# GLA diagonal as a product of q and k summed by matmuls with ones, output projection side by side, FFN groups of 16

## The chip, the cores and the metric

One core of a Trainium2 chip. The metric is the time of one execution on the device, in microseconds (us). TensorE (PE) does matmuls, VectorE (DVE) and ScalarE (ACT) element work, GpSimd (POOL) a few fills and a DMA queue, SyncE (SP) the main DMA queue.

## The reference

One layer of a hybrid decoder on x of 512 tokens and width 2048, in float32:

```python
h = rmsnorm(x); parts = split(h @ w_in)      # three head groups read the same h
mix = concat(gmlp(..), diff_attention(..), gla(..))   # 512 + 768 + 768
x = x + mix @ w_out
gate, up = split(rmsnorm(x) @ w_ffn_in)      # hidden width 5632
x = x + (silu(gate) * up) @ w_ffn_out
y = rmsnorm(x)

def gla(q, k, v, ...):                       # 4 heads, dk = 96, dv = 192, chunks of 64
    g = log_sigmoid(gate_code @ gate_w2 + gate_b) / 16
    b = cumsum(g)                            # inside a chunk
    A[i, j] = sum_d q[i, d] * k[j, d] * exp(b[i, d] - b[j, d])   # j <= i
    S = diag(exp(b_last)) @ S + (k * exp(b_last - b)).T @ v
    o = (q * exp(b)) @ S_before + A @ v
```

On the diagonal, i = j, the exponential is 1, and A[i, i] is the plain sum of q[i, d] * k[i, d] over d.

## The kernel before

Activations lie transposed, features on partitions and the 512 tokens along the row. Each float32 factor of a large product is split into a high part rounded to the fp32r format (a cast on ACT) and a low rest (a subtraction on DVE). `mm3` then makes three fp32r matmuls of each step: hi with hi, hi with lo, lo with hi.

The stages follow each other on PE. First comes the input projection (`wsr`, `wsg`, `wsd`, `b` and others are its PSUM tiles), between whose matmuls the mixers are woven in: each GLA head (`gla(h)`) and each attention head is a generator, and `pe.tick()` runs the next piece of one when the PE time estimated since its last `yield` is over. PE takes its instructions in the order in which this program writes them while `pe.held` is set. A piece's operations on ACT and DVE are written at the same point, and those queues are in order too.

In `gla(h)`, `z` is the gate's product on PE. ACT makes `ab` from it in three steps (Abs, Exp, Ln), DVE forms `pre` from `ab` and clears `suf`. After `yield 4.0` come the four matmuls of `A{h}d`, 128x128 each, of k against q: only their diagonals are used, picked into `at` by a predicated copy. Then `factors` doubles a step size from 1 to 256; its first exp is `c` from `pre`, its product with q or k is on DVE, and its sums go into `suf` and `pre`. q and k themselves are the tiles `gqk`.

The output projection (`wo_half`) runs over two halves of T (th), 16 blocks n of 128 outputs, and two halves of the 16 blocks k of `mix`; its weights are split into `wh_o` and `wl_o`, its operands are `mxs`, the split `mix`. `wo_out` adds x and keeps the sum. The loads of x for it go over SP's queue. The first LEAD = 4 blocks n have their first weight half done ahead.

The first FFN product uses a scheme with 7 products in place of 8 (`sx`, `bx`, `bz` and the like are PSUM tiles of it and of the next). The second runs over 44 hidden blocks in five parts: `rest` over 3, `second` over a group of 14, `rest` over 3, `second` over another 14, and `last` over 10. `second` makes, for each of 8 pairs q of output blocks, 7 products, each a sum over 7 pairs of hidden blocks at 3 matmuls of 256 columns. `last` takes its blocks plainly, for 10 output blocks n at 512 columns and for the last 6 in two halves of 256. `load_ops(g)` loads and splits the operands of a group, which were stored in DRAM by the first product.

Of the kernel before, what the change touches and what calls it, by code (L numbers as in the profile page):

```python
# [16 lines left out]
P = 128  # L17
# [7 lines left out]
GP = 7  # L25
R0 = (0, 1, 2)
S0 = 3
R1 = (31, 32, 33)
S1 = 17
R2 = tuple(range(34, 44))  # L30
KORDER = [*R0, *range(S0, S0 + 14, 2), *range(S0 + 1, S0 + 14, 2), *R1, *range(S1, S1 + 14, 2),
          *range(S1 + 1, S1 + 14, 2), *R2]
# [13 lines left out]

def group_of(j):
    return 0 if S0 <= j < S0 + 14 else 1 if S1 <= j < S1 + 14 else None
# [40 lines left out]
def trunk_kernel(  # L89
# [86 lines left out]
    def square_x(k):  # L176
        xt = mix[:, k]
        if k == 0:
            act.activation(sqa, xt, AF.Square)
        else:  # L180
            sq = t2(f"sq{k}")
            act.activation(sq, xt, AF.Square)
            dve.tensor_add(sqa, sqa, sq)

    def xstat(src, width, blocks, evac, name, first=False):
        for b, (c0, cw) in enumerate(blocks):
# [4 lines left out]
            for kn in steps:  # L191
# [22 lines left out]
                if first and k0 in (8, 16):  # L214
                    for k in range(k0 - 8, k0):
                        square_x(k)
# [72 lines left out]
    for h in (1, 2, 4, 8, 16, 32, 64):  # L289
# [9 lines left out]
        masks[h] = m  # L299
    one1 = mp.tile([P, 1], F32, name="one1")  # L300
# [66 lines left out]
    def gla(h, q, k):  # L367
# [12 lines left out]
        dve.memset(suf, 0.0)  # L380
        yield 4.0
# [5 lines left out]
        qh, kh = q[:DK], k[:DK]  # L387
        pa = ps(f"A{h}d")
        for i in range(4):
            sl = slice(i * P, i * P + P)  # L390
            sx = slice((i ^ 2) * P, (i ^ 2) * P + P)
            pe.matmul(pa[:, sl], lhsT=kh[:, sl], rhs=qh[:, sx], start=True, stop=True)
# [275 lines left out]
    mxs = operand("mxs")  # L668

    def split_mix(ks):  # L670
        for k in ks:
            hi, lo = (mxs[w][SLOT[k] // 8][:, SLOT[k] % 8] for w in range(2))
            act.copy(hi, mix[:, k])
            dve.tensor_sub(lo, mix[:, k], hi.bitcast(F32))

    wob, wqs = {}, []

    def wo_half(n, th, hf):
        hs = HALF[th]
        if hf == 0:  # L680
            wob[n] = big.tile([P, T], F32, tag="b", name=f"wo{n}_{th}")[:, :TH]
        wh, wl = split_w(wout[n, hf].rearrange("p k c -> p (k c)"), 1024, f"o{n}_{th}{hf}",
                         None if hf == 0 or pe.held else wqs[0].tile([P, 1024], F32, tag="raw", bufs=3, name=f"w2o{n}_{th}"))
        for kk in range(8):
# [4 lines left out]
            mm3(wob[n], wh[:, c], wl[:, c], mxs[0][k // 8][:, k % 8, hs], mxs[1][k // 8][:, k % 8, hs],  # L689
                i == 0, i == KT - 1)  # L690
# [15 lines left out]
    wqs.append(wq)  # L706
# [35 lines left out]
    def rms2(th):  # L742
# [7 lines left out]
             9: lambda: op_pair(2, b21)}  # L750
    def wo_out(n, th):
        hs = HALF[th]
        xr = wq.tile([P, 4, TH], F32, tag="s", bufs=2, name=f"xr{n}_{th}")
        nc.sync.dma_start(xr[:, 0], xT[:, n, hs])
        xn = xr[:, 0]
        dve.tensor_add(xn, wob[n], xn)
# [8 lines left out]
    for th in range(2):  # L765
        for n in range(0 if th else LEAD, KT):
            if th == 0 and n == LEAD:
                for m in range(LEAD):
                    wo_half(m, 0, 1)
                    wo_out(m, 0)  # L770
            if th == 1 and n in early:
                early[n]()
            for hf in range(2):
                wo_half(n, th, hf)
            wo_out(n, th)
# [75 lines left out]
    class Unit(Products):  # L851
        def __init__(self, j):
# [8 lines left out]
            pr, pos = (j + 1) // 2, (j + 1) % 2  # L861
# [50 lines left out]
        def p4(self):  # L912
# [9 lines left out]
            elif (self.j + 1) % 2:  # L922
# [50 lines left out]
    def load_rest(js):  # L973
        for i, j in enumerate(js):
            st = stage()
            pool.dma_start(st, actd[j])
            if len(js) == 3:
                hi, lo = ([fops[PORDER[2 * i + w]][:, 7, h] for h in range(2)] for w in range(2))
            else:
                hi, lo = (fops[PORDER[e // 8]][:, e % 8] for e in (2 * i, 2 * i + 1))  # L980
                act.copy(hi, st)
                dve.tensor_sub(lo, st, hi.bitcast(F32))
                acts[j] = (hi, lo)
                continue
            for h in range(2):
                act.copy(hi[h], st[:, h])
                dve.tensor_sub(lo[h], st[:, h], hi[h].bitcast(F32))
# [240 lines left out]
```

## Time and profile before

| | |
|---|---|
| three runs | 2123.96, 2125.35, 2126.82 us; median 2125.35 |
| profiled execution | 2125.52 us, span 2123.5 us, mean granted clock 0.997 |
| busy share of the span | PE 99%, DVE 75%, ACT 50%, POOL 5% |

The span is the stretch from the first to the last recorded work; the execution's own time has some 2 us more around it. Busy PE counts matmuls alone; their weight loads are shown apart (PEld) and run beside them. The granted clock is a share of TensorE's full speed.

### The profile page before, as it was taken

To read this page: it belongs to the slowest core of one execution; us is meant where nothing else is said; L and a number is where in the kernel's file an instruction comes from. 1 tells how busy PE (TensorE), PEld (TensorE's weight loads), DVE (VectorE), ACT (ScalarE), POOL (GpSimd) and SP (SyncE) were. 2 spreads that over 40 slices of the span, in tenths; PEclk is the share of its full clock that TensorE was granted. 3 is DMA by queue.
4 is the path that set the end of the run, shared out by engine and by line. 5 is a ranking of instruction groups with operands and counts; after the bars stand their busy time and mean duration, and the time that the engine had idled before them with its cause. 6 is when DMAs were issued, how large, how long until landed. Compare 5 with 4: busy or idle time off the path is not lost.

```text
span 2123.5 us, 33149 instructions
## 1 busy us (share of the span) xinstructions
PE 2104.5 (99%) x13210; PEld 1911.7 (90%) x13210; DVE 1584.0 (75%) x2181; ACT 1059.7 (50%) x1505; POOL 100.8 (5%) x186
## 2 busy tenths in 40 slices
PE   9999999999999999999999999999999999999997
PEld 8988899888899999888888888888888999999987
DVE  6444655566565779988988888888888788888646
ACT  6334455566655555445445544444546533433444
POOL 3000000000000000000000000000001100100000
PEclk9999999999999999999999999999999999999999
DMA  6332223222277765344444334334335644633436
GB/s 211 85 108 80 73 74 92 70 75 74 80 231 231 228 196 160 124 136 135 148 134 143 125 120 145 126 122 134 115 110 169 201 137 143 202 105 105 116 99 191
DMA packets 94683, 284.33 MB, mean 134 GB/s; under 512 B 11089, under 2 KB 29697, under 8 KB 94529
## 3 DMA queue, kind: packets, MB, share of 16 engines
q1 hardware_dynamic: 81728, 236.88, 36.0%
q0 software_dynamic: 11584, 44.57, 6.2%
q8 instruction: 104, 1.70, 0.3%
q10 hardware_dynamic: 1216, 0.76, 0.1%
q14 instruction: 51, 0.41, 0.1%
HBM read 256.74 MB, written 25.43 MB: 133 GB/s over the span
## 4 chain that ended last, share of the span: by engine, by line
PE 95%; DVE 2%; issue 1%; ACT 1%; DMA 1%; DVEq 0%; POOL 0%; POOLq 0%; ACTq 0%
PE bx L67 21%; PE bz L67 11%; PE wo L67 8%; PE sx L67 8%; PE wsd L67 6%; PE by L67 5%; PE wsg L67 4%; PE sz L67 4%; PE fb_None L67 3%; PE b L67 3%; PE c L67 3%; PE rb L67 2%; PE a L67 2%; PE wsr L67 2%; PE fb L67 2%; PE sy L67 2%
## 5 line engine op out<-in xcount | busy, mean ns | idle before, releaser
L67 PE MATMUL bx<-op,fh 128*128 128x512 f32 x1344 | 478.0, 395 | 0.0
L67 PE MATMUL bx<-op,fl 128*128 128x256 f32 x1344 | 379.3, 282 | 0.4 <-DVE fl L805 0.4
L67 PEld LDWEIGHTS bx<-op,fh 128*128 128x128 f32 x1344 | 252.4, 188 | 58.8
L804 ACT CAST fh<-s 128x1024 fp32r<-128x1024 f32 x168 | 177.0, 1053 | 197.6 <-PE by L67 63.8
L67 PEld LDWEIGHTS bx<-op,fl 128*128 128x128 f32 x1344 | 253.1, 188 | 0.8 <-DVE fl L805 0.8
L67 PE MATMUL bz<-op,fh 128*128 128x512 f32 x672 | 240.5, 396 | 0.0
L805 DVE TENSOR_TENSOR fl<-s,fh 128x1024 fp32r<-128x1024 f32 x168 | 204.5, 1218 | 47.9 <-ACT fh L804 47.9
L804 ACT CAST fh<-f 128x1024 fp32r<-128x1024 f32 x126 | 132.5, 1052 | 170.0 <-PE bx L67 85.9
L67 PE MATMUL bz<-op,fl 128*128 128x256 f32 x672 | 189.5, 282 | 0.2 <-DVE fl L805 0.2
L67 PE MATMUL wo<-mxs,wh_o 128*128 128x256 f32 x1024 | 184.1, 283 | 0.0
L805 DVE TENSOR_TENSOR fl<-f,fh 128x1024 fp32r<-128x1024 f32 x126 | 153.7, 1220 | 16.7 <-ACT fh L804 16.7
L67 PE MATMUL sx<-fop,wh_s 128*128 128x256 f32 x896 | 162.0, 282 | 0.0
L67 PEld LDWEIGHTS wo<-mxs,wh_o 128*128 128x128 f32 x1024 | 158.5, 190 | 0.1
L67 PEld LDWEIGHTS bz<-op,fh 128*128 128x128 f32 x672 | 126.2, 188 | 30.5
L67 PE MATMUL wo<-mxs,wl_o 128*128 128x256 f32 x512 | 144.9, 283 | 2.0 <-DVE wl_o L152 2.0
L67 PEld LDWEIGHTS sx<-fop,wh_s 128*128 128x128 f32 x896 | 137.9, 189 | 0.2 <-issue 0.2
L67 PEld LDWEIGHTS bz<-op,fl 128*128 128x128 f32 x672 | 126.7, 188 | 0.5 <-DVE fl L805 0.5
L67 PE MATMUL sx<-fop,wl_s 128*128 128x256 f32 x448 | 126.1, 281 | 0.0
L67 PE MATMUL wsd<-xs,wh_d 128*128 128x512 f32 x384 | 122.9, 401 | 0.0
L67 PE MATMUL by<-op,fh 128*128 128x512 f32 x336 | 119.9, 397 | 0.0
L67 PEld LDWEIGHTS wo<-mxs,wl_o 128*128 128x128 f32 x512 | 97.2, 190 | 2.2 <-DVE wl_o L152 2.2
L67 PE MATMUL by<-op,fl 128*128 128x256 f32 x336 | 94.2, 280 | 0.0
(406 smaller groups left out, 4769.5 us busy)
## 6 DMA issues: line engine op xcount, KB each, us to landing
f<-wf SPq DMA_DIRECT2D x168, 512.0 KB, 3.9
w_o<-wout SPq DMA_DIRECT2D x32, 512.0 KB, 4.2
w2o<-wout SPq DMA_DIRECT2D x32, 512.0 KB, 3.9
sraw<-wf SPq DMA_DIRECT2D x32, 448.0 KB, 3.9
sw<-wf SPq DMA_DIRECT2D x32, 448.0 KB, 4.2
opd<-tmp POOLq DMA_DIRECT2D x14, 896.0 KB, 4.1
w_d<-wst SPq DMA_DIRECT2D x24, 512.0 KB, 3.5
w_g<-wst SPq DMA_DIRECT2D x16, 512.0 KB, 3.5
```

What stands on the lines that cost most here:

```text
L67: self.note(self.tc.nc.tensor.matmul(out, lhsT=lhsT, rhs=rhs, **k), out, rhs)
L804: act.copy(wh, a)
L805: dve.tensor_sub(wl, a, wh.bitcast(F32))
```

## The change

There are three parts and some small ones. In each GLA head the diagonal becomes an elementwise product: DVE multiplies k and q into `ab`, ACT casts that to `qkh`, DVE subtracts to get the rest `qkl`, and two fp32r matmuls of 512 columns with a matrix of ones (`onesr`) sum each over the 96 partitions. In the output projection hi and lo of an operand lie beside each other, so that one matmul of 512 columns does hi with hi and hi with lo in two halves of a PSUM tile, and one of 256 does lo with hi; `wo_out` adds both halves. Its loads of x go to POOL's queue, one turn ahead. In the second FFN product the groups have 16 blocks instead of 14, and `last` 6 instead of 10; operands and weights lie in other buffers for it. The squares of x at the start are made in smaller portions and kept in program order.

```diff
-GP = 7
+GP = 8
 R0 = (0, 1, 2)
 S0 = 3
-R1 = (31, 32, 33)
-S1 = 17
-R2 = tuple(range(34, 44))
-KORDER = [*R0, *range(S0, S0 + 14, 2), *range(S0 + 1, S0 + 14, 2), *R1, *range(S1, S1 + 14, 2),
-          *range(S1 + 1, S1 + 14, 2), *R2]
+R1 = (19, 20, 21)
+S1 = 22
+R2 = tuple(range(38, 44))
+KORDER = [*R0, *range(S0, S0 + 16, 2), *range(S0 + 1, S0 + 16, 2), *R1, *range(S1, S1 + 16, 2),
+          *range(S1 + 1, S1 + 16, 2), *R2]
...
+SQUARES = {4: (0, 3), 6: (3, 6), 8: (6, 8), 10: (8, 10), 12: (10, 12), 14: (12, 14), 16: (14, 16)}
...
-                if first and k0 in (8, 16):
-                    for k in range(k0 - 8, k0):
-                        square_x(k)
+                for k in range(*SQUARES.get(k0, (0, 0)) if first else (0,)):
+                    square_x(k)
...
+    onesr = mp.tile([P, P], F32R, name="onesr")
+    act.activation(onesr, ident, AF.Copy, scale=0.0, bias=1.0)
...
         dve.tensor_sub(pre, pre, ab)
         dve.memset(suf, 0.0)
+        qh, kh = q[:DK], k[:DK]
+        qkh = mp.tile([P, T], F32R, tag="t", bufs=7, name=f"qkh{h}")[:DK]
+        qkl = mp.tile([P, T], F32R, tag="t", bufs=7, name=f"qkl{h}")[:DK]
+        for e in range(2):
+            dve.tensor_mul(ab[:, HALF[e]], kh[:, HALF[e]], qh[:, HALF[1 - e]])
+        act.copy(qkh, ab)
+        dve.tensor_sub(qkl, ab, qkh.bitcast(F32))
         yield 4.0
         at = mp.tile([P, 10 * P], F32, tag="at", bufs=2, name=f"at{h}")
         atd = at[:, :T].rearrange("p (a b) -> p a b", b=P)
         pool.memset(at[:, :T], 0.0)
-        qh, kh = q[:DK], k[:DK]
         pa = ps(f"A{h}d")
-        for i in range(4):
-            sl = slice(i * P, i * P + P)
-            sx = slice((i ^ 2) * P, (i ^ 2) * P + P)
-            pe.matmul(pa[:, sl], lhsT=kh[:, sl], rhs=qh[:, sx], start=True, stop=True)
+        pe.matmul(pa, lhsT=onesr[:DK], rhs=qkh, start=True, stop=False)
+        pe.matmul(pa, lhsT=onesr[:DK], rhs=qkl, start=False, stop=True)
...
-    mxs = operand("mxs")
+    mxs = [opp.tile([P, 4, 2, 2, TH], F32R, tag=f"o{i}", name=f"mxs{i}") for i in (0, 2, 1, 3)]
     def split_mix(ks):
         for k in ks:
-            hi, lo = (mxs[w][SLOT[k] // 8][:, SLOT[k] % 8] for w in range(2))
-            act.copy(hi, mix[:, k])
-            dve.tensor_sub(lo, mix[:, k], hi.bitcast(F32))
-    wob, wqs = {}, []
-    def wo_half(n, th, hf):
-        hs = HALF[th]
+            hi, lo = (mxs[SLOT[k] // 4][:, SLOT[k] % 4, :, w] for w in range(2))
+            src = mix[:, k].rearrange("p (h t) -> p h t", h=2)
+            act.copy(hi, src)
+            dve.tensor_sub(lo, src, hi.bitcast(F32))
+    wob = {}
+    def wo_half(n, th, hf, own=None):
         if hf == 0:
-            wob[n] = big.tile([P, T], F32, tag="b", name=f"wo{n}_{th}")[:, :TH]
+            wob[n] = big.tile([P, T], F32, tag="b", name=f"wo{n}_{th}")
         wh, wl = split_w(wout[n, hf].rearrange("p k c -> p (k c)"), 1024, f"o{n}_{th}{hf}",
-                         None if hf == 0 or pe.held else wqs[0].tile([P, 1024], F32, tag="raw", bufs=3, name=f"w2o{n}_{th}"))
+                         own and own.tile([P, 1024], F32, tag="raw", bufs=3, name=f"w2o{n}_{th}"))
         for kk in range(8):
             pe.tick()
             i = 8 * hf + kk
             k = SLOT[ORDER[i]]
             c = slice(kk * P, kk * P + P)
-            mm3(wob[n], wh[:, c], wl[:, c], mxs[0][k // 8][:, k % 8, hs], mxs[1][k // 8][:, k % 8, hs],
-                i == 0, i == KT - 1)
+            both = mxs[k // 4][:, k % 4, th]
+            pe.matmul(wob[n], lhsT=wh[:, c], rhs=both, start=i == 0, stop=False, skip_group_check=True)
+            pe.matmul(wob[n][:, :TH], lhsT=wl[:, c], rhs=both[:, 0], start=False, stop=i == KT - 1, skip_group_check=True)
...
+    xrs = {}
+    def wo_x(n, th):
+        xrs[n, th] = wq.tile([P, 4, TH], F32, tag="ld", bufs=3, name=f"xr{n}_{th}")
+        pool.dma_start(xrs[n, th][:, 0], xT[:, n, HALF[th]])
     def wo_out(n, th):
         hs = HALF[th]
-        xr = wq.tile([P, 4, TH], F32, tag="s", bufs=2, name=f"xr{n}_{th}")
-        nc.sync.dma_start(xr[:, 0], xT[:, n, hs])
+        xr = xrs.pop((n, th))
         xn = xr[:, 0]
-        dve.tensor_add(xn, wob[n], xn)
+        dve.tensor_add(xn, wob[n][:, :TH], xn)
+        dve.tensor_add(xn, wob[n][:, TH:], xn)
...
-    for th in range(2):
-        for n in range(0 if th else LEAD, KT):
-            if th == 0 and n == LEAD:
-                for m in range(LEAD):
-                    wo_half(m, 0, 1)
-                    wo_out(m, 0)
-            if th == 1 and n in early:
-                early[n]()
-            for hf in range(2):
-                wo_half(n, th, hf)
-            wo_out(n, th)
+    turns = [(n, th) for th in range(2) for n in range(KT)]
+    wo_x(*turns[0])
+    for i, (n, th) in enumerate(turns):
+        if i + 1 < len(turns):
+            wo_x(*turns[i + 1])
+        if th == 1 and n in early:
+            early[n]()
+        for hf in range(1 if i < LEAD else 0, 2):
+            wo_half(n, th, hf, wq if hf and i >= LEAD else None)
+        wo_out(n, th)
...
             if len(js) == 3:
-                hi, lo = ([fops[PORDER[2 * i + w]][:, 7, h] for h in range(2)] for w in range(2))
+                ra = wq.tile([P, 2, 2, TH], F32R, tag="ld", bufs=3, name=f"ra{j}")
+                hi, lo = ra[:, 0], ra[:, 1]
...
     def load_ops(g):
         for pi in PORDER:
-            for i, w, tg, bufs in ((0, 4, "ld", 3), (4, 3, "s", 2)):
-                st = wq.tile([P, 4, TH], F32, tag=tg, bufs=bufs, name=f"so{g}{pi}{i}")[:, :w]
-                pool.dma_start(st, opd[g][i:i + w, :, pi - 1].rearrange("a p t -> p a t"))
-                hi, lo = (fops[pi][:, i:i + w, x] for x in range(2))
+            for i, tg, bufs in ((0, "raw", 3), (4, "s", 2)):
+                st = wq.tile([P, 1024], F32, tag=tg, bufs=bufs, name=f"so{g}{pi}{i}").rearrange("p (a t) -> p a t", t=TH)
+                pool.dma_start(st, opd[g][i:i + 4, :, pi - 1].rearrange("a p t -> p a t"))
+                hi, lo = (fops[pi][:, i:i + 4, x] for x in range(2))
...
+    LW, KT_F = len(R2) * P, len(KORDER)
     def last(n, th):
         hs = slice(0, T) if th is None else HALF[th]
         b = p2.tile([P, T], F32, tag="b", name=f"fb{n}_{th}")[:, :hs.stop - hs.start]
-        for ci in range(2):
-            w = wp.tile([P, 1024], F32, tag="w", name=f"fw{n}_{th}{ci}")[:, :5 * P]
-            nc.sync.dma_start(w, wf2[n, :, 34 + 5 * ci:39 + 5 * ci].rearrange("p k c -> p (k c)"))
-            wh, wl = w_split(w, 5 * P, f"f{n}_{th}{ci}")
-            for kk in range(5):
-                c = slice(kk * P, kk * P + P)
-                ah, al = acts[R2[5 * ci + kk]]
-                if th is not None:
-                    ah, al = ah[:, th], al[:, th]
-                mm3(b, wh[:, c], wl[:, c], ah, al, ci == 0 and kk == 0, ci == 1 and kk == 4)
+        if th != 1:
+            w = wp.tile([P, 1024], F32, tag="w", name=f"fw{n}")[:, :LW]
+            nc.sync.dma_start(w, wf2[n, :, KT_F - len(R2):].rearrange("p k c -> p (k c)"))
+        if th is None:
+            wh, wl = w_split(w, LW, f"f{n}")
+        else:
+            m = n - WIDE
+            both = fops[PORDER[2 + m // 2]].rearrange("p k w t -> p (k w t)")
+            wh, wl = (both[:, (2 * (m % 2) + x) * LW:(2 * (m % 2) + x + 1) * LW] for x in range(2))
+            if th == 0:
+                act.copy(wh, w)
+                dve.tensor_sub(wl, w, wh.bitcast(F32))
+        for kk, j in enumerate(R2):
+            c = slice(kk * P, kk * P + P)
+            ah, al = acts[j]
+            if th is not None:
+                ah, al = ah[:, th], al[:, th]
+            mm3(b, wh[:, c], wl[:, c], ah, al, kk == 0, j == R2[-1])
```

The first place is `A0d` in PE's queue, in the middle of the projection `wsr`. Before:

```order
L67 MATMUL wsr_1230<-xs_102,wh_r_1_1274 128x512
L67 MATMUL wsr_1230<-xs_104,wh_r_1_1274 128x512
L67 MATMUL wsr_1230<-xs_102,wl_r_1_1275 128x512
L67 MATMUL A0d<-gqk_1162,gqk_1227 128x128 x4
L67 MATMUL wsr_1230<-xs_102,wh_r_1_1274 128x512
```

After:

```order
L70 MATMUL wsr_1232<-xs_102,wh_r_1_1282 128x512
L70 MATMUL wsr_1232<-xs_104,wh_r_1_1282 128x512
L70 MATMUL wsr_1232<-xs_102,wl_r_1_1283 128x512
L70 MATMUL A0d<-qkh_1259,onesr 128x512
L70 MATMUL A0d<-qkl_1260,onesr 128x512
L70 MATMUL wsr_1232<-xs_102,wh_r_1_1282 128x512
```

The matmuls of `A0d` stand at the same place, but read `qkh` and `qkl` in place of q and k.

The second place is the same piece of the program in ACT's queue, after:

```order
L379 ACTIVATE ab_1252<-z_1250,gbs 96x512
L380 ACT_TABLE_LOAD
L380 ACTIVATE ab_1252<-ab_1252 96x512
L381 ACT_TABLE_LOAD
L381 ACTIVATE ab_1252<-ab_1252,one_561 96x512
L154 CAST wh_r_1_1381<-w_r_1_1379 128x1024
L431 ACT_TABLE_LOAD
L431 ACTIVATE c_0_1295<-pre_1248 96x256
L390 CAST qkh_1259<-ab_1252 96x512
L435 ACTIVATE c_0_1334<-suf_1249 96x128x2
```

The cast to `qkh` is the one new row; it stands behind the three steps of the gate, a weight cast, a table load and the first exp of `factors`.

The third place is DVE's queue there. Before:

```order
L379 TENSOR_TENSOR pre_1246<-pre_1246,ab_1250 96x512
L432 TENSOR_TENSOR suf_1247<-suf_1247,pre_1246 96x128 x2
L152 TENSOR_TENSOR wl_r_1_1376<-w_r_1_1373,wh_r_1_1375 128x1024
L393 COPY_PREDICATED at_1281<-ident,A0d 128x512
L429 TENSOR_TENSOR c_0_1289<-c_0_1289,gqk_1162 96x256
```

After:

```order
L383 TENSOR_TENSOR pre_1248<-pre_1248,ab_1252 96x512
L389 TENSOR_TENSOR ab_1252<-gqk_1229,gqk_1164 96x256 x2
L437 TENSOR_TENSOR c_0_1295<-c_0_1295,gqk_1164 96x256
L440 TENSOR_TENSOR suf_1249<-suf_1249,pre_1248 96x128 x2
L155 TENSOR_TENSOR wl_r_1_1382<-w_r_1_1379,wh_r_1_1381 128x1024
L391 TENSOR_TENSOR qkl_1260<-ab_1252,qkh_1259 96x512
L401 COPY_PREDICATED at_1289<-ident,A0d 128x512
```

The product of k and q follows `pre`; the product of the first `c`, which before came after the copy from `A0d`, now stands ahead of `suf` and the split `wl_r`, and `qkl` behind all of them.

## Rows read from the trace of the kernel before

**Rows 1.** The page, busy time of each engine, its share and instructions.

```profile
PE 2104.5 (99%) x13210; PEld 1911.7 (90%) x13210; DVE 1584.0 (75%) x2181; ACT 1059.7 (50%) x1505; POOL 100.8 (5%) x186
```

**Rows 2.** Waits of PE, first and last of twelve: total us, times, longest.

```profile
PE wo L67 <- DVE wl_o L152: 2.0, 1, 2.0
...
PE c L67 <- ACT rs L225: 0.2, 1, 0.2
```

**Rows 3.** The chain that ended last: start us, us, engine, tile, line, count.

```profile
685.26 85.44 PE wo L67 x720
...
836.41 5.63 PE bx L67 x32
...
1714.93 4.99 PE sx L67 x42
...
1997.15 68.47 PE fb_None L67 x300
2065.62 25.01 PE fb L67 x210
```

**Rows 4.** Timeline of ACT and DVE, heads 1 to 3: start us, us, instruction.

```profile
232.73 0.44 ACT L423 ACTIVATE c<-pre 96x256 f32<-96x256 f32 x1
...
289.23 0.43 DVE L429 TENSOR_TENSOR c<-c,gqk 96x256 f32<-96x256 f32 x1 [0.41 <-ACT c L423]
289.57 0.49 DVE L432 TENSOR_TENSOR suf<-suf,pre 96x128 f32<-96x128 f32 x2
289.98 0.95 DVE L202 TENSOR_TENSOR wl_b<-w_b,wh_b 128x768 fp32r<-128x768 f32 x1
...
346.38 0.95 DVE L202 TENSOR_TENSOR wl_b<-w_b,wh_b 128x768 fp32r<-128x768 f32 x1
```

**Rows 5.** Timeline of PE, head 0.

```profile
148.47 0.39 PE L67 MATMUL z<-gct,w2c 96*96 96x512 f32 x1
...
152.89 1.06 PE L67 MATMUL A0d<-gqk,gqk 96*128 96x128 f32 x8
...
153.70 0.71 PE L67 MATMUL wsr<-xs,wh_r 128*128 128x512 f32 x2
```

**Rows 6.** Timeline of ACT, head 0.

```profile
152.84 0.72 ACT L377 ACTIVATE ab<-ab,one 96x512 f32<-96x512 f32 x1
...
153.47 1.04 ACT L151 CAST wh_r<-w_r 128x1024 fp32r<-128x1024 f32 x1
...
155.82 0.44 ACT L423 ACTIVATE c<-pre 96x256 f32<-96x256 f32 x1
```

**Rows 7.** Timeline of DVE, head 0.

```profile
153.60 0.69 DVE L379 TENSOR_TENSOR pre<-pre,ab 96x512 f32<-96x512 f32 x1 [2.54 <-ACT ab L377]
...
154.32 0.49 DVE L432 TENSOR_TENSOR suf<-suf,pre 96x128 f32<-96x128 f32 x2
...
154.73 1.21 DVE L152 TENSOR_TENSOR wl_r<-w_r,wh_r 128x1024 fp32r<-128x1024 f32 x1
...
155.87 0.74 DVE L393 COPY_PREDICATED at<-ident,A0d 128x512 f32<-128x512 uint32 x1
```

**Rows 8.** Timeline of PE, what follows the diagonal in heads 1 to 3.

```profile
230.61 0.72 PE L67 MATMUL wsg<-xs,wh_g 128*128 128x512 f32 x2
...
285.78 0.42 PE L67 MATMUL b<-wh_b,xs 128*128 128x384 f32 x1
...
342.17 0.42 PE L67 MATMUL b<-wh_b,xs 128*128 128x384 f32 x1
```

**Rows 9.** Windows: us, busy PE, PEld, DVE, ACT, POOL, granted clock, DMA share, GB/s.

```profile
590.20:592.10 1.90, 0.00 (x0) 0.00 (x0) 1.90 (x4) 0.47 (x1) 0.00 (x0) 1.00 0.95 358
592.30:595.70 3.40, 3.40 (x18) 3.40 (x19) 2.75 (x4) 0.98 (x1) 0.00 (x0) 0.53 0.99 369
596.00:599.40 3.40, 3.40 (x31) 3.40 (x30) 1.23 (x1) 1.10 (x2) 0.00 (x0) 1.00 0.50 196
```

**Rows 10.** Timeline of ACT, the weight cast of the blocks behind the waiting `wo`.

```profile
583.99 1.05 ACT L151 CAST wh_o<-w_o 128x1024 fp32r<-128x1024 f32 x1 [0.36 <-ACT mxs L673]
```

More of the change, by code (lines that the diff above doesn't have):

```diff
@@ L44 @@
 WIDE = 10
+SQUARES = {4: (0, 3), 6: (3, 6), 8: (6, 8), 10: (8, 10), 12: (10, 12), 14: (12, 14), 16: (14, 16)}
 def group_of(j):
-    return 0 if S0 <= j < S0 + 14 else 1 if S1 <= j < S1 + 14 else None
+    return 0 if S0 <= j < S0 + 2 * GP else 1 if S1 <= j < S1 + 2 * GP else None
 class Queue:
@@ L178, in square_x @@
         if k == 0:
-            act.activation(sqa, xt, AF.Square)
+            tc.keep_in_program_order(act.activation(sqa, xt, AF.Square))
         else:
             sq = t2(f"sq{k}")
-            act.activation(sq, xt, AF.Square)
+            tc.keep_in_program_order(act.activation(sq, xt, AF.Square))
             dve.tensor_add(sqa, sqa, sq)
@@ L705, in trunk_kernel @@
     wq = tc.alloc_tile_pool(name="wq", bufs=1)
-    wqs.append(wq)
     x1 = keep.tile([P, KT, T], F32, tag="k", name="x1")
@@ L860, in __init__ @@
             self.z5, self.gt = tmp[:, o + 4 * TH:o + 6 * TH], tmp[:, o + 6 * TH:o + 8 * TH]
-            pr, pos = (j + 1) // 2, (j + 1) % 2
+            pr, pos = divmod(j + (1 if j < S1 else 2), 2)
+            self.pos = pos
             self.pr = tmp[:, (pr % 2) * PAIR:(pr % 2 + 1) * PAIR].rearrange("p (s t) -> p s t", t=TH)
@@ L921, in p4 @@
                 pool.dma_start(actd[self.j], self.ac)
-            elif (self.j + 1) % 2:
+            elif self.pos:
                 pr = self.pr
@@ L977, in load_rest @@
             if len(js) == 3:
-                hi, lo = ([fops[PORDER[2 * i + w]][:, 7, h] for h in range(2)] for w in range(2))
+                ra = wq.tile([P, 2, 2, TH], F32R, tag="ld", bufs=3, name=f"ra{j}")
+                hi, lo = ra[:, 0], ra[:, 1]
             else:
                 hi, lo = (fops[PORDER[e // 8]][:, e % 8] for e in (2 * i, 2 * i + 1))
[L981 to L987, printed above, removed]
+            act.copy(hi, st)
+            dve.tensor_sub(lo, st, hi.bitcast(F32))
             acts[j] = (hi, lo)
@@ L1019, in rest @@
                         ah, al = acts[js[kk]]
-                        mm3(b[:, HALF[h]], wh[:, c], wl[:, c], ah[h], al[h], kk == 0, kk == kw - 1)
+                        mm3(b[:, HALF[h]], wh[:, c], wl[:, c], ah[:, h], al[:, h], kk == 0, kk == kw - 1)
                 if base == 0:
@@ L1080, in trunk_kernel @@
             load_rest(R1)
-    rest(R1, 17)
+    rest(R1, 19)
     load_ops(1)
     for q in range(KT // 2):
-        second(q, 20)
+        second(q, 22)
     load_rest(R2)
```

## The prediction

> **What bounds the kernel now.** I read the page first, for the share of each engine: PE is busy 99% of the span, DVE 75%, ACT 50% [rows 1]. So the time is the sum of the durations of the PE instructions, plus the few places where PE stands still. Next the list of what PE waited for: its longest wait is 2.0 us, for `wl_o` on DVE as the output projection begins, and the twelve entries go down from there to 0.2, under 10 us in all [rows 2]. Third the chain that ended last: it is nearly all PE, with long unbroken runs, so that the mean of one matmul can be divided out of it [rows 3]: `wo` 85.44 us / 720 = 0.1187 us for 256 columns, `bx` 5.63 us / 16 pairs = 0.352 us for one of 512 and one of 256, `sx` 4.99 / 42 = 0.1188, `fb_None` 68.47 / 300 = 0.2282 for 512 columns, `fb` 25.01 / 210 = 0.1191. An edit is therefore worth what it changes in matmul columns at these prices, and loses whatever makes PE wait. The profiled execution took 2125.52 us with a span of 2123.5; the median of the three runs is 2125.35, so I sum against 2125.5 and treat that as the median too. Less than 0.2% (4 us) is about what a measurement of this kernel cannot tell from no change.
>
> **Output projection side by side.** There are 16 blocks n, 2 halves of T and 16 blocks k: 512 steps. Before, a step is three matmuls of 256: 1536 x 0.1187 = 182.3 us. After, it is one of 512 (hi and lo beside each other) and one of 256, the same pair of shapes as `bx`: 512 x 0.352 = 180.1. That is -2.2 us. The second sum is joined by one more add out of PSUM per (n, half), 128x256. The nearest rows are DVE operations of 96x256 at 0.43 [rows 4], so 32 x 0.43 = 14 us more on an engine that is busy 75% in all; `wob` has four PSUM buffers, so a turn may end late without holding PE. I take 0. The loads of x move from SP's queue to POOL's, one turn ahead of use, and POOL is busy 5% [rows 1]: 0. The 2.0 us wait for `wl_o` stands behind the splits of `mxs` on ACT and DVE; there is as much to split in the new layout, and the first matmul that waits is again one of a second weight half, so I leave it where it is, with 0 to 4 us as bounds (the wait gone, or doubled with its clock, below).
>
> **FFN groups of 16.** The two grouped parts of the second FFN product (`second`) take 8 pairs instead of 7: 8 q x 2 groups x 7 products x 3 matmuls = 336 more of 256 columns, at 0.1191: +40.0 us. The last part (`last`) falls from 10 blocks to 6: for the 10 wide n 10 x 4 x 3 = 120 matmuls of 512 less, 120 x 0.2282 = 27.4, and for the 6 narrow n 6 x 2 x 4 x 3 = 144 of 256 less, 144 x 0.1191 = 17.2. Net 40.0 - 27.4 - 17.2 = -4.5 us. The first FFN product is unchanged. What goes with it runs beside PE: two more pair sums per group on DVE, and operand loads of eight slots a product instead of seven, now in buffers that the weight loads of `second` share. These loads fall into the part `rest`, in which PE has its own work (16 blocks x 2 halves x 9 = 288 matmuls of 0.119, 34 us); I take 0, and up to 4 us for each group if a shared buffer comes free late.
>
> **The GLA diagonal.** Before, `A{h}d` is four fp32 matmuls of 128 columns straight from q and k, which have long been ready. In head 0 they stand at 152.89 and the main stream goes on at 153.70: 0.81 us [rows 5]. After, it is two fp32r matmuls of 512 columns, 2 x 0.228 = 0.46 us: -0.35 us a head, if nothing is waited for. But their operands `qkh` and `qkl` are now made from `ab`, and `ab` is the buffer of the gate chain (Abs, Exp, Ln), which may only be overwritten once `pre` has been formed from it. The two matmuls stand at the same place in PE's order as the four did, 18 matmuls behind `z`. I follow the chain behind that place. The last ACT step on `ab` (Ln) runs 152.84 to 153.56, with A0d already due [rows 6]. DVE forms `pre` from 153.60 [rows 7]. Behind it the product k q is two DVE operations of 0.43, and could be done by about 155. However, the cast to `qkh` stands on ACT behind the cast of `wh_r`, a table load and the first exp `c`, which ends at 155.82 + 0.44 = 156.26 [rows 6]. And `qkl` stands on DVE behind the product that needs that exp, behind `suf`, and in heads 0 and 1 behind the split `wl_r`.
>
> So, head 0: exp done 156.26, product to `suf` +0.34 (head 2 shows such a step, 289.23 to 289.57 [rows 4]), `suf` to `wl_r` 154.73 - 154.32 = +0.41, `wl_r` to the next DVE operation 155.87 - 154.73 = +1.14 [rows 7], `qkl` itself +0.69 as `pre`, the same 96x512 subtraction: 158.84. Then +0.23 for the second matmul: the main stream goes on at 159.07 instead of 153.70: **+5.4 us**. Head 1: exp ends 232.73 + 0.44 = 233.17, the same +2.58 gives 235.75, +0.23 = 235.98 against 230.61 [rows 4, 8]: **+5.4**. Head 2: here the DVE operation after `suf` starts at 289.98 and is a weight split that in the new order stands behind `qkl`; so 289.98 + 0.69 + 0.23 = 290.90 against 285.78 [rows 4, 8]: **+5.1**. Head 3: 346.38 + 0.69 + 0.23 = 347.30 against 342.17: **+5.1**. Sum **+21.0 us**, the old matmuls taken out and the new ones in. PE runs its matmuls in the order they stand in: while it waited from 590.2 to 592.1, no matmul ran at all [rows 9], although `wh_o`, the operand of the next blocks, had been cast since 585.04 [rows 10]. All that is queued behind A0d on PE (the `wsr` matmuls of the projection, whose operands are there) waits with it.
>
> The Trainium skill, page "TensorE: Matmul & The Clock Gate", section "Step-by-step: what each phase is for", says that MATMULs stay in program order and only the loading of weights is pulled ahead; that speaks against this change. By that rule the stall stays whole; the trace agrees, with 0 matmuls in 590.2 to 592.1.
>
> **The clock after a wait.** After the 2.0 us wait the granted clock was 0.53 over 592.3 to 595.7, near the lower of the two levels (1.2 instead of 2.4 GHz): 18 matmuls there, 31 in the equally long stretch after [rows 9]. That is 13 x 0.119 = 1.55 us lost. The new waits are some 5 us each, longer than that one. I price each at the same 1.55: 4 x 1.55 = **+6.2 us**, with 0 and twice that as bounds.
>
> The same page, section "Why this matters for your kernels", warns of PE-idle gaps between bursts of matmuls, after which the clock returns to its lower level. [...]
>
> **The small edits.** The squares of x at the start are kept in program order and spread over the loads; ACT and DVE have slack there, and PE has its loaded matmuls as cover: 0, at most 0.5 either way. `onesr` is one ACT operation, off the path.
>
> **Sum:** 2125.5 - 2.2 - 4.5 + 21.0 + 6.2 = **2146.0 us**.
>
> **Rivals.**
> *Waits without the lower clock.* If the waits fall so that the chip keeps the upper level, 6.2 goes: 2139.8. For it: the clock was 0.53 after only one wait, and I have no other of that length. Against it: the new waits are more than twice as long. Chance 0.17.
> *Waits, and a new stall besides.* The operand loads of the FFN groups wait for a buffer shared with weight loads (up to 4 us each), or the wait at the output projection doubles: +6 on top, about 2152. For it: 8 slots are loaded instead of 7 through fewer buffers. Against it: the part `rest` covers 34 us of loading. Chance 0.12.
> *Faster: the operands are in time.* Place: the two matmuls `A{h}d` on PE. If the product and its split do not wait for the gate chain, the diagonal gains 4 x 0.35 = 1.4 instead of losing 27: 2125.5 - 2.2 - 4.5 - 1.4 = 2117.4. The change saves 8.1 us in all without waits, so the point that decides is a wait of 8.1 / 4 = 2.0 us a head, lower clock included; my chain says 5.1 to 5.4 and has to be wrong by 3 us in every head. For it: q and k are ready early. Against it: the product is written into `ab`, and both engines take their queues in order. Chance 0.06.
> *My forecast*, 2142 to 2150 (each wait off by up to 0.5 us, each clock loss by up to 0.5): chance 0.65.
>
> **How the numbers follow.** The likeliest case gives 2146.0. The range 2135 to 2155 holds it with its bounds, the case without lower clock and most of the new stall; it leaves out the faster rival and the upper ends of the unknown costs. Faster: only the last rival, 0.05. Within 0.2% (2121 to 2130): waits of 2 to 3 us a head, 0.02. Slower 0.93.
>
> **What would show it.** In the profile after: `A0d` to `A3d` as four waits of PE, each 5 to 6 us in the list of waits, on DVE's `qkl`; DVE's `qkl` ending near 158.8 in head 0; a granted clock under 1.00 in the microseconds after each; the run of `wo` shorter by 2.2; `second` longer by 40, `last` shorter by 44.5. The prediction is wrong if `qkl` is early, if matmuls behind `A0d` run before it, or if the waits of PE at the FFN groups grow.

## The result and the profile after

The change makes the kernel slower: 2149.82 us (median of 4 runs, 2149.54 to 2153.26) against 2126.09 for the kernel before on the same chip, a ratio of 1.0114, 95% interval 1.0102 to 1.0126. The forecast was 2146.0, range 2135 to 2155. The profiled execution has a span of 2148.3 us, 24.8 more than before. Of all executions counted below one, of the output projection alone, took 4469.8 us and stays out of its ratio.

The page of the changed kernel, beside [rows 1]; "issue" in its fourth part is time in which an engine waited for nothing that the profile shows:

```profile
PE 2107.4 (98%) x12746; PEld 1892.3 (88%) x12746; DVE 1611.9 (75%) x2195; ACT 1057.3 (49%) x1472; POOL 112.8 (5%) x212
...
PE 82%; issue 11%; DMA 3%; ACT 2%; DVE 2%; POOL 0%; SPq 0%; DVEq 0%; POOLq 0%; ACTq 0%
```

PE has 464 instructions fewer and is busy 2.9 us longer, and the span is 24.8 us longer: about 22 us are idle time that was not there. Its list of waits, beside [rows 2]:

```profile
PE A3d L70 <- ACT qkh L390: 4.7, 1, 4.7
PE A2d L70 <- ACT qkh L390: 4.7, 1, 4.7
PE A0d L70 <- ACT qkh L390: 3.7, 1, 3.7
PE A1d L70 <- ACT qkh L390: 3.7, 1, 3.7
PE bz L70 <- DVE fl L818: 2.3, 1, 2.3
PE wo L70 <- ACT wh_o L154: 1.6, 1, 1.6
PE A1d L70 <- DVE qkl L391: 1.3, 1, 1.3
PE A0d L70 <- DVE qkl L391: 1.3, 1, 1.3
```

Four waits of about 5 us stand at the diagonal of the four heads, first for `qkh`, in heads 0 and 1 then for `qkl`. The fifth row, `bz` for `fl`, was 0.2 us before; the forecast had nothing there.

The timeline of head 0, beside [rows 5 to 7] (rows of `wsr` and those of the weight loads left out):

```profile
153.61 0.72 ACT L381 ACTIVATE ab<-ab,one 96x512 f32<-96x512 f32 x1
154.24 1.03 ACT L154 CAST wh_r<-w_r 128x1024 fp32r<-128x1024 f32 x1
154.37 0.69 DVE L383 TENSOR_TENSOR pre<-pre,ab 96x512 f32<-96x512 f32 x1 [2.54 <-ACT ab L381]
155.09 0.76 DVE L389 TENSOR_TENSOR ab<-gqk,gqk 96x256 f32<-96x256 f32 x2
155.29 1.28 ACT L431 ACT_TABLE_LOAD   x1
156.58 0.43 ACT L431 ACTIVATE c<-pre 96x256 f32<-96x256 f32 x1
156.92 0.60 ACT L390 CAST qkh<-ab 96x512 fp32r<-96x512 f32 x1
157.04 0.42 DVE L437 TENSOR_TENSOR c<-c,gqk 96x256 f32<-96x256 f32 x1 [1.20 <-ACT c L431]
157.38 0.48 DVE L440 TENSOR_TENSOR suf<-suf,pre 96x128 f32<-96x128 f32 x2
157.57 0.79 PE L70 MATMUL A0d<-qkh,onesr 96*128 96x512 f32 x1 [3.75 <-ACT qkh L390]
157.79 1.22 DVE L155 TENSOR_TENSOR wl_r<-w_r,wh_r 128x1024 fp32r<-128x1024 f32 x1
...
158.93 0.68 DVE L391 TENSOR_TENSOR qkl<-ab,qkh 96x512 fp32r<-96x512 f32 x1
...
159.66 0.80 PE L70 MATMUL A0d<-qkl,onesr 96*128 96x512 f32 x1 [1.30 <-DVE qkl L391]
...
160.25 1.06 PE L70 MATMUL wsr<-xs,wh_r 128*128 128x512 f32 x2
```

The product is done at 155.85. The cast of it waits on ACT behind a table load and the first exp until 156.92, its rest on DVE behind three operations until 158.93. `qkl` ends at 159.61; the forecast had 158.84, and this kernel reaches the place 0.77 us later (`z` at 149.24 for 148.47). The windows of that place (us, busy PE, PEld, DVE, ACT, POOL, granted clock, DMA share, GB/s):

```profile
153.80:157.50 3.70, 0.02 (x1) 0.00 (x0) 1.90 (x5) 3.67 (x5) 0.00 (x0) 0.79 0.00 0
157.57:160.20 2.63, 1.33 (x2) 0.79 (x3) 2.63 (x6) 0.67 (x2) 0.00 (x0) 0.50 0.01 3
160.25:163.60 3.35, 3.35 (x11) 2.67 (x10) 3.00 (x10) 1.00 (x3) 0.00 (x0) 0.62 0.51 157
```

The clock falls while PE waits (0.79 of full speed as a mean), is at the lower level (0.50, half of full speed) as the two matmuls run, and returns within the third window.

The runs of the chain that answer to [rows 3]:

```profile
710.09 84.26 PE wo L70 x480
...
2067.34 40.85 PE fb_None L70 x180
```

A step of the projection is now 84.26 / 240 = 0.351 us; `fb_None` has 180 matmuls instead of 300 at 0.227. A table of where stages begin, read from the timelines (first or last matmul of the tile, us), shows where the 24.6 us are:

| | before | after | later by |
|---|---|---|---|
| `z` of head 0 | 148.47 | 149.24 | 0.8 |
| first `wo` | 583.98 | 611.09 | 27.1 |
| last `wo` | 770.42 | 794.06 | 23.6 |
| first `rb` (second FFN product) | 1646.48 | 1674.54 | 28.1 |
| first `fb_None` | 1996.99 | 2067.18 | 70.2 |
| first narrow `fb` | 2065.46 | 2108.03 | 42.6 |
| last matmul ends | 2114.15 | 2138.72 | 24.6 |

The first stage loses 26.3 us, the projection gains 3.5, the first FFN product loses 4.4, the groups lose 42.1 and `last` gains 45.6.

### The profile page after: what moved, and what is told of

Same layout as the page of the kernel before. It is cut to its first block, busy times and chain, and to the rows that moved or that the text cites. A ratio compares the mean times of both kernels' runs of the same rounds, so it can differ in the third digit from the quotient of the medians.

```text
span 2148.3 us, 32040 instructions
## 1 busy us (share of the span) xinstructions
PE 2107.4 (98%) x12746; PEld 1892.3 (88%) x12746; DVE 1611.9 (75%) x2195; ACT 1057.3 (49%) x1472; POOL 112.8 (5%) x212
## 4 chain that ended last, share of the span: by engine, by line
PE 82%; issue 11%; DMA 3%; ACT 2%; DVE 2%; POOL 0%; SPq 0%; DVEq 0%; POOLq 0%; ACTq 0%
PE bx L70 17%; PE bz L70 8%; PE wo L70 8%; PE sx L70 7%; PE wsd L70 6%; PE by L70 4%; PE wsg L70 4%; PE sz L70 4%; PE c L70 3%; PE b L70 3%; PE wsu L70 2%; PE a L70 2%; PE wsr L70 2%; PE fb_None L70 2%; PE sy L70 2%
## 5 line engine op out<-in xcount | busy, mean ns | idle before, releaser
L70 PE MATMUL sx<-fop,wh_s 128*128 128x256 f32 x1024 | 185.1, 282 | 0.9 <-DVE acc L1058 0.8
L70 PE MATMUL wo<-mxs,wh_o 128*128 128x512 f32 x512 | 180.3, 394 | 1.6 <-ACT wh_o L154 1.6
L70 PEld LDWEIGHTS sx<-fop,wh_s 128*128 128x128 f32 x1024 | 157.8, 189 | 1.2 <-issue 1.2
L70 PE MATMUL sx<-fop,wl_s 128*128 128x256 f32 x512 | 144.3, 282 | 0.0
L70 PEld LDWEIGHTS wo<-mxs,wh_o 128*128 128x128 f32 x512 | 96.2, 188 | 24.0 <-ACT wh_o L154 1.9
L70 PEld LDWEIGHTS sx<-fop,wl_s 128*128 128x128 f32 x512 | 96.8, 189 | 0.0
```

The source lines that it names most:

```text
L70: self.note(self.tc.nc.tensor.matmul(out, lhsT=lhsT, rhs=rhs, **k), out, rhs)
```

## The experiments

**The old diagonal in the changed kernel.**

```diff
-        pe.matmul(pa, lhsT=onesr[:DK], rhs=qkh, start=True, stop=False)
-        pe.matmul(pa, lhsT=onesr[:DK], rhs=qkl, start=False, stop=True)
+        for i in range(4):
+            ...
+            pe.matmul(pa[:, sl], lhsT=kh[:, sl], rhs=qh[:, sx], start=True, stop=True)
```

> The changed kernel with the four fp32 matmuls of the diagonal put back; all else of the change stays. Theory (the loss is the wait for the product in each GLA head and the lower clock after it): the first matmul of the output projection, which came 27.1 us late, comes about 0.8 us late; the time is 2149.8 - 26.3 = 2123.5 us, and A0d to A3d are no waits of PE. Rival (the other parts of the change cost a good part of the first stage, by the buffers or the kept order of the squares): 2130 or more.

Measured: 2119.88 us against 2125.33, ratio 0.9975 (0.9965 to 0.9985). The first `wo` starts at 584.26, 0.3 us later than before. So the whole loss of the first stage hangs on the diagonal; the rival falls. The time is 3.6 us below the expectation, which took the changed kernel's one profile for all other stages. In this run's profile the start is 0.5 us earlier, the projection 0.5 us shorter, and the first FFN product loses 3.2 us instead of 4.4; besides, that execution (2121.70 us) is 1.8 us above the median of the nine.

**The new diagonal alone in the kernel before.** The product, its split and the two matmuls, as in the diff above the prediction, with `onesr`.

> The kernel before with the new diagonal and nothing else of the change. Theory: the same four waits of about 5 us and the same lower clock behind each, +26.3 us: 2126.1 + 26.3 = 2152.4. Rival (the waits come about only with the other parts, through the shifted start or other buffers): under 2140.

Measured: 2154.02 against 2125.33, ratio 1.0140 (1.0125 to 1.0155); the same four waits (3.7 + 1.3, 3.7 + 1.6, 4.7, 4.7), the first `wo` 27.9 us later. The diagonal costs 28.7 us by itself, and no other part of the change is needed for it. That is 2.4 us more than the 26.3 expected; the lower clock costs more in this profile (below).

**The product ahead of the gate, in a buffer of its own.**

```diff
+        qh, kh = q[:DK], k[:DK]
+        qk = t2(f"qk{h}")[:DK]
...
+        for e in range(2):
+            dve.tensor_mul(qk[:, HALF[e]], kh[:, HALF[e]], qh[:, HALF[1 - e]])
+        act.copy(qkh, qk)
+        dve.tensor_sub(qkl, qk, qkh.bitcast(F32))
         pre, suf = g96("pre"), g96("suf")
...
-            dve.tensor_mul(ab[:, HALF[e]], kh[:, HALF[e]], qh[:, HALF[1 - e]])
-        act.copy(qkh, ab)
-        dve.tensor_sub(qkl, ab, qkh.bitcast(F32))
```

> The changed kernel with the product of q and k in a buffer of its own, made and split ahead of the gate's three steps; operations and matmuls are the same in number. Theory (PE waits because the product shares the gate's buffer and so stands behind the gate chain): no waits at A0d to A3d, the diagonal gains 0.35 us a head against the fp32 one, 2149.8 - 26.3 - 1.4 = 2122.1 us. Rival (the matmuls with ones wait for other reasons, or the extra work ahead of the gate makes the factors late and PE waits there instead): 2130 to 2150.

Measured: 2116.25 against 2125.33, ratio 0.9962 (0.9949 to 0.9975). None of the waits at the diagonal is left, and PE runs through the place, in its timeline:

```profile
153.10 0.39 PE L70 MATMUL wsr<-xs,wl_r 128*128 128x512 f32 x1
153.32 0.40 PE L70 MATMUL A0d<-qkh,onesr 96*128 96x512 f32 x1
153.56 0.39 PE L70 MATMUL A0d<-qkl,onesr 96*128 96x512 f32 x1
153.78 0.63 PE L70 MATMUL wsr<-xs,wh_r 128*128 128x512 f32 x2
```

The same operations, 33.6 us less: what costs is when the product is made. The run gives the product a buffer of its own and an earlier place at once; which of the two it needs is not separated. `A0d` takes 153.32 to 153.78, 0.46 us, where the fp32 one took 0.81. The time is 5.9 us below the expectation: 2.1 us of that are pieces of the heads that fall elsewhere (the last experiment), and the first FFN product loses 2.0 us instead of 4.4.

**Filler ahead of the diagonal.**

```diff
+        for _ in range(20):
+            tc.keep_in_program_order(nc.tensor.matmul(pa, lhsT=onesr, rhs=xs[0][0][:, 0], start=True, stop=True))
         pe.matmul(pa, lhsT=onesr[:DK], rhs=qkh, start=True, stop=False)
```

> The changed kernel with 20 fp32r matmuls of 512 columns ahead of the two of the diagonal in each head (into the same PSUM tile, overwritten afterwards; they add nothing to the result): 4.6 us of work at full speed, in place of some 5 us of waiting. Theory (of about 7 us lost in a head, 5 are the wait and 2 to 3 are the lower clock after it): the waits shrink to under 0.6 us, the clock stays at 1.00, and the time falls by 4 x 2.5 = 10 us to 2140. Rival (the clock costs nothing that would not be lost anyway, or the wait for DVE is all): 2149 to 2151.

Measured: 2136.72 against 2125.33, ratio 1.0060 (1.0045 to 1.0075); 13.1 us less than the changed kernel. Its windows at head 0 (columns as above):

```profile
154.00:158.60 4.60, 4.06 (x18) 2.95 (x16) 3.37 (x8) 3.29 (x5) 0.00 (x0) 1.00 0.00 0
159.30:162.70 3.40, 3.40 (x16) 2.75 (x16) 3.33 (x12) 1.36 (x4) 0.00 (x0) 1.00 0.47 157
```

The operands come no sooner, but the clock stays at 1.00, behind the other three diagonals too. The waits were expected under 0.6 us; they are 1.0 in heads 0 and 1 and 0.4 in heads 2 and 3. This separates the two terms. The first matmuls of `wsd`, which stand in the main stream behind the four diagonals, in the kernel before, with the filler and in the changed kernel:

```profile
357.85 0.62 PE L67 MATMUL wsd<-xs,wh_d 128*128 128x512 f32 x2
...
379.30 0.62 PE L70 MATMUL wsd<-xs,wh_d 128*128 128x512 f32 x2
...
387.18 0.62 PE L70 MATMUL wsd<-xs,wh_d 128*128 128x512 f32 x2
```

They come 21.45 us later than before with the filler and 29.33 us in the changed kernel. Less what each had lost at `z` of head 0 (0.12 and 0.77), the heads lose 21.3 us by the waits alone and 28.6 us with the lower clock; the difference, 7.2 us, is the lower clock. The other 6 us of the 13.1 lie outside the heads, 3.5 of them in the first FFN product, which loses 1.0 us in this run.

**The diagonal one piece later.**

```diff
-        pa = ps(f"A{h}d")
-        pe.matmul(pa, lhsT=onesr[:DK], rhs=qkh, start=True, stop=False)
-        pe.matmul(pa, lhsT=onesr[:DK], rhs=qkl, start=False, stop=True)
...
         c = factors(1)
         yield 6.0
+        pa = ps(f"A{h}d")
+        pe.matmul(pa, lhsT=onesr[:DK], rhs=qkh, start=True, stop=False)
+        pe.matmul(pa, lhsT=onesr[:DK], rhs=qkl, start=False, stop=True)
...
```

> The changed kernel with the two matmuls of the diagonal (and the copy behind them) written one piece later, behind the yield of 6.0 that follows the first factors; the product stays in the gate's buffer and its chain is as long as in the changed kernel. Theory (what costs is that PE, in order, stands at these two matmuls when their operands are not there): the operands come some 5.5 us after the old place and the new place is some 6 us after it, so the waits fall under 0.5 us each with no clock lost, and the time is that of the early product or up to 3 us more: 2116 to 2119. Rival (the length of the chain itself delays the head's later pieces): 2125 or more.

Measured: 2117.15 against 2127.35, ratio 0.9953 (0.9939 to 0.9968). One wait of 0.6 us at the diagonal is in its list. The product is as late as in the changed kernel (its cast starts 7.69 us after `z` of head 0, 7.68 there), and it costs next to nothing, since PE comes to it when it is there. So what costs the time in the changed kernel is neither the operations nor the length of their chain, but that PE comes to the two matmuls before their operands are there.

**The casts for the first three hidden blocks pinned.**

```diff
+            a, d = act.copy(hi, st), dve.tensor_sub(lo, st, hi.bitcast(F32))
+            if js == R0:
+                tc.keep_in_program_order(a)
+                tc.keep_in_program_order(d)
...
+        if j == 8:
+            load_rest(R0)
+        u = Unit(j)
...
-    load_rest(R0)
     rest(R0, 0)
```

> The changed kernel with the casts of the first three hidden blocks for the second FFN product pinned on ACT and DVE behind the sixth of the units that follow; before, the scheduler put the first of them on ACT ahead of an operand cast of the first FFN product, where it waited for a read back from DRAM. Theory (the 4.4 us lost between the output projection and the second FFN product in the changed kernel come from this row): that stretch is as long as before the change within 0.6 us, the wait of bz for fl (2.3 us) is gone, 2149.8 - 4.1 = 2145.7. Rival (the stall comes from the weights, which arrive at another time): 2149 to 2151.

Measured: 2148.52 against 2127.35, ratio 1.0105 (1.0089 to 1.0120). This row on ACT in the changed kernel led to it, in the timeline:

```profile
837.28 0.38 ACT L859 ACTIVATE sm<-dx 128x256 f32<-128x256 f32 x1
841.26 0.62 ACT L996 CAST ra<-st 128x512 fp32r<-128x512 f32 x1 [3.61 <-DMA st<-actd]
841.78 1.90 ACT L744 CAST op<-x 128x2048 fp32r<-128x2048 f32 x1
```

The cast of `ra` waits 3.61 us for a read back from DRAM, with the operand cast `op` behind it, and `bz` waits 2.3 us for the `fl` that comes after that. With the pin that wait of `bz` is gone (0.2 left) and the stretch loses 1.3 instead of 4.4 us. The other traces bear this out. Over the first 380 of the 4704 matmuls of the first FFN product, the seven kernels with groups of 16 and no pin lose 0.7 to 4.0 us against the kernel before (3.6 in the changed kernel); the four with the pin lose nothing, and neither do the two with groups of 14. What is left of the 4.4 us stands at the end of that product, 0.8 us without the pin and 1.2 with it.

But the time fell by 1.3 us only, within the spread of the runs, and the size of the expectation was missed. The profiled execution, 2151.53 us, is the longest of the four. In it the heads lose 30.8 us (28.6 in the changed kernel), since the clock falls later and returns later, and 2.1 us more go in the first `rest`, where the weights of `rb` come late, by 1.06 and 0.49 us, and the clock behind is at its lower level:

```profile
1694.00:1697.00 3.00, 1.45 (x10) 1.04 (x9) 2.44 (x3) 2.10 (x4) 0.00 (x0) 1.00 0.84 316
1697.00:1700.50 3.50, 3.50 (x18) 3.50 (x18) 2.90 (x3) 3.50 (x7) 0.00 (x0) 0.51 0.55 167
```

The changed kernel has two waits of 0.5 us there. The cause of these waits is not shown. A cast of a group's operands (`fop`) waited 3.34 us for its load ahead of them, but 2.94 us in the changed kernel as well, and the run of the projection alone, with groups of 14, loses 3.0 us at the same place.

**Early product and pinned casts.** The edits of the two together.

> The early product and the pinned casts together, nothing else. The early product alone had 2.0 us left over between the output projection and the second FFN product, against the kernel before; theory: 2116.3 - 1.7 = 2114.5. Rival (the casts pinned later collide with the units): 2116 or more.

Measured: 2116.66 against 2127.35, ratio 0.9952 (0.9936 to 0.9969), the same as the early product alone; the expected 1.7 us did not come. The first FFN product still loses 1.8 us, 2.0 without the pin: the stall of `bz` that the pin removes (2.3 us in the changed kernel) is not in the list of waits of the early product, so there was little to take. Of the 0.7 us that went at the start of the product, 0.6 are lost again at its end.

**The squares as before, besides.** `SQUARES` out, two portions again, not kept in order.

> As the one with the early product and the pinned casts, and the squares of x at the start again in two portions and not kept in program order. In the changed kernel the first matmuls after the start came 0.5 to 0.8 us later than before. Theory: 0.5 us faster than its neighbour, 2114.0, hardly to be told by the time alone, but z of head 0 comes 0.4 us earlier. Rival: the start varies by that much between runs of any kernel, and nothing changes.

Measured: 2116.77, ratio 0.9952 (0.9937 to 0.9967). `z` of head 0 starts at 149.13, later and not earlier than its neighbour's 148.56. Over all profiles it starts at 148.47 to 149.63 with the old squares and at 148.43 to 149.24 with the new ones: the rival, the start varies between runs, and no cost of the squares shows.

**The output projection alone in the kernel before.** The hunks on `mxs`, `wo_half`, `wo_x` and `wo_out`.

> The kernel before with the output projection side by side (and the loads of x on the other queue) and nothing else. By the forecast's own term the 512 steps at 0.352 us in place of 1536 matmuls at 0.1187 give -2.2 us; the traces of the kernels with the whole change show the stretch of wo 3.5 to 4.3 us shorter, as the waits at its beginning shrink too. Theory: -3.5 to -4.3, that is 2122.5 us. Rival (the second add out of PSUM and the other loads hold up what follows): 2126 or more.

Measured: 2122.67 against 2126.38, ratio 0.9981 (0.9972 to 0.9990). That is -3.7 us, as the traces had it. The 2.0 us wait for `wl_o` is one of 1.6 for `wh_o` now, and the clock stays at 1.00 behind it.

**The groups of 16 alone in the kernel before.** The hunks on `GP`, `R0` to `S1`, `Unit`, `load_rest`, `load_ops` and `last`.

> The kernel before with the groups of 16 in the second FFN product, its buffers and loads, and nothing else. By the forecast -4.5 us: 336 matmuls of 0.1191 more, 120 of 0.2282 and 144 of 0.1191 less. The row on ACT that holds up an operand cast of the first FFN product comes with this part; it costs 0.3 to 4 us. Theory: -4.5 + 2 = 2123.6 us. Rival (the loads of eight slots hold up each group): 2128 or more.

Measured: 2126.91 against 2126.38, ratio 0.9999 (0.9989 to 1.0009), with runs from 2121.57 to 2130.43. That is 3.3 us above the expectation and below the rival's 2128. Its profiled execution was one of the long ones, 2129.54 us: the first FFN product loses 4.0 us there, the first `rest` another 2.3. In the first of these stretches a cast of `ra` waits on ACT again, and PE then waits 1.9 us for `fh`, the cast behind it:

```profile
855.76 0.62 ACT L986 CAST ra<-st 128x512 fp32r<-128x512 f32 x1 [5.25 <-DMA st<-actd]
```

**The same with the pinned casts.** The edit on `load_rest(R0)` as above.

> The groups of 16 alone, with the casts of the first three hidden blocks pinned behind the sixth unit. The groups alone came out level with the kernel before: their matmuls are 5 us less, but in the profile 4.0 us more went between the output projection and the second FFN product, and 2.3 at the beginning of the latter. Theory (the unpinned row makes most of the first of these): the 4.0 fall to about 1, the time to 2126.9 - 3 = 2124. Rival (the stall moves to the beginning of the second FFN product, as with the whole change): 2126 to 2127.

Measured: 2121.64 against 2126.45, ratio 0.9978 (0.9967 to 0.9988). In its profile the first FFN product loses nothing (the first `rb` is at 1647.39, 0.9 later than before, as the first `wo` is already). The groups are worth -4.8 us, as the forecast had them, and most of what had hidden that are these casts: the pin took 4.0 us out of the first FFN product. The first `rest` loses 0.2 us here; the rival falls.

**The old diagonal with the new one's count of time.** The line is shown against the first experiment.

```diff
             pe.matmul(pa[:, sl], lhsT=kh[:, sl], rhs=qh[:, sx], start=True, stop=True)
+        pe.t -= 0.425
```

> The changed kernel with the old diagonal, and the PE time that the program counts for it lowered by 0.425 us a head, to what it counts for the new one; the work is the same, only where later pieces of the heads fall between the matmuls of the projection changes. Theory (1.7 us of the gain of the early product over the old diagonal come from pieces that stand elsewhere): the waits of pt for st (1.1 us) and of sc for mix (0.4 us) in the first stage are gone, and the time is 2119.9 - 1.7 = 2118.2. Rival (they come from the diagonal's own operations): no change, 2119.9.

Measured: 2117.13 against 2126.38, ratio 0.9961 (0.9949 to 0.9972). The waits of `pt` for `st` and of `sc` for `mix` are gone, and the first `wo` is 2.3 us earlier than with the old diagonal alone. In its profile 2.1 us come back between the heads and the first `wo`, and the same 2.1 to 2.2 us come back there in every kernel with the new diagonal, and in none with the old diagonal and its old count. So part of what the early product gains is that pieces of the heads fall elsewhere between the matmuls, not that the new diagonal is cheaper. Against this run the early product is 2.0 us shorter in the first stage of its profile, but only 0.9 us faster in the median, within the spread.

## Why the prediction was right, step by step

**PE is the bound, and takes its matmuls in order.** Right. The operands of the `wsr` behind A0d were there, and none of them ran between 153.82 and 157.57. By the rule of the Trainium skill (page "TensorE: Matmul & The Clock Gate", section "Step-by-step: what each phase is for"), matmuls are not pulled ahead; the trace of the changed kernel agrees, with 3.75 us of waiting in head 0. With the diagonal moved one piece later, one wait of 0.6 us is left in all four heads.

**The waits, +21.0.** Measured 21.3, from the run with filler. The chain held operation by operation: cast behind the exp, `qkl` behind `wl_r` in heads 0 and 1; less the 0.77 us that this kernel is late at `z`, `qkl` ends at 158.84 in head 0, as the forecast had it. The list of waits looks otherwise than forecast: the longer wait of each head is the one for `qkh` (3.7 or 4.7 us), where the forecast named `qkl` for all four.

**The lower clock, +6.2.** Measured 7.2, by the same run, 1.8 a head for 1.55. The profiles of two other kernels with the same waits lose more in the heads, 29.6 (diagonal alone) and 30.8 (pinned casts) for 28.6, so that 8.2 and 9.5 would be the clock there; the bound was 12.4. The price of 1.55 came from one stretch behind one wait, so that it came this near is partly luck. The rival without it falls: the clock was 0.50 behind every one of the four waits.

**What the forecast left out of the first stage.** Up to `wsd` the changed kernel is 29.3 us late, at the first `wo` 27.1: 2.2 us come back before the projection. The program counts less PE time for the new diagonal, so that later pieces fall elsewhere and two waits (1.1 and 0.4 us before) are gone; the last experiment gets 2.1 us from the count alone.

**Output projection, -2.2.** The step was right, 0.351 us each for the forecast 0.352 (512 of these are 180.2, so the term is -2.1); the whole measured -3.5 in the changed kernel and -3.7 alone. What was off is the wait at its start, put down as unchanged: it shrank from 2.0 to 1.6 us, and the clock behind it stayed at 1.00, where the forecast's own row of before has 0.53. A new wait of 0.7 us for `wl_o` takes part of that back in the changed kernel.

**FFN groups, -4.5.** Right as work, -4.8 alone with the cast out of the way. In the profile of the changed kernel the groups cost 42.1 and `last` saves 45.6, which is -3.5. The term that failed is "The first FFN product is unchanged", put at 0: it lost 4.4 us. The casts for the first three hidden blocks have other tiles, outside the groups' operands; the first of them stands on ACT at 841.26 now (the row of `ra` above). Before, it stood at the end of that product:

```profile
1631.16 0.71 ACT L986 CAST fop<-st 128x256 fp32r<-128x256 f32 x2
```

So these casts now come ahead of work that is needed, which costs 3.6 of the 4.4. That they come early because their new tiles are free early is likely, but no run shows it alone. The second rival had a stall at the groups' operand loads; in the changed kernel the first `rest` loses 0.25 us, so it did not come.

**The sum.** By the profiles:

| | forecast | measured |
|---|---|---|
| start | 0 | +0.8 |
| waits at the diagonal | +21.0 | +21.3 |
| lower clock behind them | +6.2 | +7.2 |
| rest of the first stage | 0 | -2.2 |
| output projection | -2.2 | -3.5 |
| first FFN product | 0 | +4.4 |
| groups and `last` | -4.5 | -3.5 |
| sum | +20.5 | +24.5 |

The two large terms were forecast by their mechanism. That the sum came within 4 us is in part luck: terms that came out 7.5 us higher (4.4 of them the first FFN product) stand against 3.5 us lower (the rest of the first stage and the projection). Why the casts of `ra` cost from 0.7 to 4.0 us in kernels that differ elsewhere is not settled.

The version to keep is one whose diagonal does not wait: the early product, 2116.25 us, is faster than both kernels, and the piece moved back, 2117.15, does as well. So does the old diagonal with the lower count, 2117.13: how much of the gain the new diagonal itself has is not clear of the spread.

## What to carry to other kernels

Before work moves off a full in-order engine onto idle ones, follow each new operand through the queues to the instruction that needs it; here the product was written behind a chain that has nothing to do with it, into that chain's buffer. If it comes late, make it earlier or take it later: here either took back some 33 us without one operation less. And when work moves to other buffers, look where the scheduler places it: it can come early, in front of what is needed.

## What the runs showed of the hardware that was not expected

In heads 0, 2 and 3 the lower clock came while PE was still waiting: 0.79 as a mean over 153.80 to 157.50, 0.50 in the 2.6 us after. In head 1 it was 1.00 until 241.00, near the end of the wait, and 0.50 from 241.40. In the run with the pinned casts it was 1.00 through the whole first wait of head 0 and fell only behind it; there the heads lost 2.3 us more:

```profile
153.30:156.90 3.60, 0.02 (x1) 0.02 (x1) 2.00 (x6) 3.50 (x5) 0.00 (x0) 1.00 0.00 0
157.70:160.30 2.60, 1.33 (x3) 1.14 (x4) 2.32 (x5) 0.45 (x1) 0.00 (x0) 0.50 0.09 24
```

The length of a wait alone does not decide. Waits of 1.0 us before the second matmul, in the run with filler, left the clock at 1.00 in the window behind; the single wait of 2.3 us in the changed kernel was followed by 0.70 and 0.80:

```profile
845.20:847.50 2.30, 0.00 (x0) 0.00 (x0) 2.30 (x4) 0.58 (x1) 0.54 (x1) 1.00 0.00 0
847.50:850.90 3.40, 3.37 (x14) 2.96 (x15) 3.40 (x4) 1.05 (x1) 1.09 (x2) 0.70 0.29 78
850.90:854.30 3.40, 3.40 (x17) 2.91 (x17) 3.00 (x4) 2.76 (x4) 0.00 (x0) 0.80 0.48 129
```

But a wait of 2.4 us in the run with the old diagonal left it at 1.00, and waits of 1.06 and 0.49 us in the run with the pinned casts were followed by 0.51 (above):

```profile
853.00:855.40 2.40, 0.00 (x0) 0.03 (x1) 2.11 (x4) 2.29 (x3) 0.00 (x0) 1.00 0.00 0
855.40:858.80 3.40, 3.40 (x19) 3.02 (x20) 3.37 (x5) 0.59 (x2) 0.00 (x0) 1.00 0.40 154
```
